# Encoder layer with a mixture of experts on one core: gate weights applied at the experts' eviction, second gather added in the DMA, last norm in two DVE operations

## The chip, the cores and the metric

One core of one Trainium2 chip. The metric is the device time of one execution in microseconds; lower is better. Times of before are the median of three runs, and one further execution was profiled.

## The reference

For 2048 tokens of width 1024, in fp32, one layer with two sub-layers:

```
x = layernorm(x, ln0)
x = layernorm(ALPHA * x + mixer(x), ln1)
group = argmax(x @ w_rg);  two best of the 8 experts in that group
w = softmax(two logits) * softmax(groups)[group]
ffn[token] = sum over its 2 experts of  w * ((silu(x @ w1[e]) * (x @ w3[e])) @ w2[e])
ple = sigmoid(x @ w_ple_gate + b) * (p @ w_ple_proj)
out = layernorm(ALPHA * x + ffn + ple, ln2)
```

There are 32 experts; each token goes to two. The mixer is a gated short convolution and centred pooling between an input and an output projection.

## The kernel before

Every fp32 product is made of three matmuls on TensorE (`mm3`, L222 to L224): each operand is split into a high half (ACT cast, L332) and a low half (subtraction, mostly on DVE, L333), and high x high, high x low and low x high are added up in PSUM. Weights stream through two pools of 128x1024 slots in SBUF, called RB and RY (one allocator, SR); split operands lie in FB.

The work runs in stages. First the norm and the mixer, up to some 560 us. Then the output projection, the second norm and the router of the 16 token tiles. Then, up to a loop at some 730 us, the "embed" products (the `ple` term, `embed_tile`) of six tiles run on TensorE while `dispatch` works out where each token's rows go. Then come the 32 experts, up to some 1450 us, and last the tail: the embed products of the other ten tiles (the list END), beside which `fetch` gathers each token's two expert rows and `finish` forms the last norm.

`dispatch` (L909 to L1014) counts the rows of each expert, ranks experts by size, and gives every (token, choice) a slot number SLI, split into block BLK and position POS. To turn this into a table "which token is in block b at position q" it multiplies matrices: "place" (L1000, one-hot in position, eight tiles in 1024 columns) times "num" (L991, one-hot in block, times the token number at L993), 32 matmuls on TensorE (L1005) that add up in one PSUM bank. TBI and TBH are the tables read from it; gathers of the experts' inputs (L1332, by POOL's queue) use them. Where a token has its rows in the result is known from SLI.

The experts write their results, unweighted, to `yd` in DRAM: ACT copies PSUM to SBUF (L1631; for a half block DVE adds the two halves) and a DMA on POOL's queue stores it.

In the tail, `fetch` (L1735 to L1749) loads for the six early tiles the sum of the other terms (`based`) and gathers two slots of 128x1024 for each tile, from `yd`, with two indirect DMAs on POOL's queue. `finish` then runs for 14 tiles: two weighted additions on DVE (L1783, with the gate weights GW, the second also summing the row), the mean's sign and scale on POOL (L1789), Square with a sum on ACT (L1791), the variance, its power -1/2 and the bias on POOL (L1793 to L1795), the normalisation on ACT (L1797), the multiplication by the norm's weight on DVE (L1798), and the addition of its bias on POOL, or for a quarter of the tiles on DVE (L1799). `finish_last` does the last two tiles in halves, by another form of the norm (`ln_apply`, L328 and L329). L1238, L1243 and L1252 evict the embed products on DVE. The output DMAs stand on ACT's queue.

The order of instructions on every engine is set when the kernel is built, by a planner with costs of its own; generators (`yield`) offer their work to it in pieces. So a change of an operation can move others.

## Time and profile before

| | before |
|---|---|
| median of 3 runs | 1617.14 us (1616.31 to 1617.79) |
| profiled execution | 1620.22 us, its span 1618.6 us |
| TensorE busy | 1550.0 us, 96% of the span |
| DVE, ACT, POOL busy | 1158.9, 792.2, 490.8 us |
| mean granted TensorE clock | 0.982 |
| DMA | 430.63 MB, 266 GB/s |

The busy share of an engine tells only which one has no room; what a stage costs is read from its waits and from the timeline. A matmul's row gives its whole duration, 0.39 us for 512 columns; since matmuls overlap, the distance of two starts (0.23 us) is what one costs. PEclk is the share of full speed that TensorE's clock was granted.

### The profile page before, as it was taken

What the parts mean: (1) busy time and instruction counts of PE and PEld (TensorE: products, weight loads), DVE (VectorE), ACT (ScalarE), POOL (GpSimd) and SP (SyncE); (2) the same over time, 40 slices, a digit from 0 to 9 for tenths busy, and PEclk for the clock granted to TensorE, in tenths of its full rate; (3) what the DMA queues carried; (4) which work ended last, traced back from release to release, by engine and by line L of the source; (5) the groups of instructions that cost most, each with busy time, mean ns of one, the idle gap of its engine ahead of it and who ended that gap; (6) DMA issues with size and microseconds to landing.
All of it is one profiled execution on the core that took longest, in us unless ns stands there. A gap on an engine that the chain in (4) does not pass through costs nothing.

```text
span 1618.6 us, 22474 instructions
## 1 busy us (share of the span) xinstructions
PE 1550.0 (96%) x7770; PEld 1306.8 (81%) x7771; DVE 1158.9 (72%) x1492; ACT 792.2 (49%) x1027; POOL 490.8 (30%) x683
## 2 busy tenths in 40 slices
PE   6999999999999999998999999999999999999895
PEld 5887878887878887777988998988888888878774
DVE  6777484345666667767888878878888767767796
ACT  7343242113111124137778777777787766652332
POOL 3455673441133215110313101111111111007763
PEclk9999999999999999999999999999999999999987
DMA  6547159886386536459788998999998987987961
GB/s 208 183 147 224 63 171 310 335 301 199 108 268 212 169 107 255 139 201 358 280 332 320 401 378 316 355 369 345 355 359 325 329 306 282 384 328 281 357 216 65
DMA packets 205757, 430.63 MB, mean 266 GB/s; under 512 B 19144, under 2 KB 70904, under 8 KB 205640
## 3 DMA queue, kind: packets, MB, share of 16 engines
q1 hardware_dynamic: 162096, 292.33, 50.5%
q0 software_dynamic: 35024, 125.65, 21.1%
q10 hardware_dynamic: 8520, 11.18, 2.0%
q8 instruction: 62, 1.02, 0.2%
q14 instruction: 55, 0.45, 0.1%
HBM read 331.95 MB, written 97.16 MB: 265 GB/s over the span
## 4 chain that ended last, share of the span: by engine, by line
PE 45%; POOL 4%; issue 2%; DVE 2%; ACT 1%; DMA 1%; POOLq 0%; ACTq 0%; DVEq 0%
PE PS L1519 10%; PE PS L222 10%; PE PS L224 10%; PE PS L223 10%; PE PS L339 2%; PE PS L1465 1%; PE PS L1466 1%; POOL RY L1799 1%; PE PS L1589 1%; POOL RY L1746 1%; POOL rstd L1794 1%; POOL rstd L1793 0%; DMA RB<-based 0%; PE PS L1383 0%; POOL RB L1746 0%
## 5 line engine op out<-in xcount | busy, mean ns | idle before, releaser
L223 PE MATMUL PS<-FB 128*128 128x512 f32 (+1 forms) x1356 | 527.3, 389 | 5.5 <-DVE FB L333 5.5
L222 PE MATMUL PS<-FB 128*128 128x512 f32 (+1 forms) x1276 | 497.5, 393 | 15.6 <-DVE FB L333 10.5
L224 PE MATMUL PS<-FB 128*128 128x512 f32 (+1 forms) x1276 | 495.0, 389 | 3.0 <-DVE FB L333 2.9
L333 DVE TENSOR_TENSOR FB<-RY,FB 128x1024 fp32r<-128x1024 f32 x243 | 292.8, 1229 | 53.5 <-ACT FB L332 36.9
L223 PEld LDWEIGHTS PS<-FB 128*128 128x128 f32 x1356 | 258.3, 190 | 56.7 <-DVE FB L333 7.0
L222 PEld LDWEIGHTS PS<-FB 128*128 128x128 f32 x1276 | 242.9, 191 | 65.0 <-DVE FB L333 12.0
L224 PEld LDWEIGHTS PS<-FB 128*128 128x128 f32 x1276 | 242.7, 190 | 52.6 <-DVE FB L333 4.2
L333 DVE TENSOR_TENSOR FB<-RB,FB 128x1024 fp32r<-128x1024 f32 x201 | 241.8, 1218 | 59.3 <-ACT FB L332 46.1
L332 ACT CAST FB<-RY 128x1024 fp32r<-128x1024 f32 x247 | 252.7, 1051 | 60.9 <-PE PS L223 22.9
L332 ACT CAST FB<-RB 128x1024 fp32r<-128x1024 f32 x205 | 211.0, 1049 | 122.9 <-PE PS L223 41.3
L1519 PE MATMUL PS<-FB 128*128 128x296 f32 (+15 forms) x1280 | 175.4, 297 | 6.4 <-ACT FB L332 5.7
L1519 PEld LDWEIGHTS PS<-FB 128*128 128x128 f32 x1280 | 171.3, 191 | 7.8 <-issue 5.9
L332 ACT CAST FB<-PS 128x1024 fp32r<-128x1024 f32 (+9 forms) x142 | 81.7, 592 | 137.6 <-PE PS L339 83.3
L333 DVE TENSOR_TENSOR FB<-PS,FB 128x1024 fp32r<-128x1024 f32 (+9 forms) x142 | 96.0, 689 | 62.2 <-ACT FB L332 61.8
L223 PE MATMUL PS<-FB,FY 128*128 128x512 f32 x264 | 104.1, 394 | 0.0
L1332 POOL DMA_INDIRECT RY<-x1d,TBI x22 | 47.8, 2175 | 173.1 <-DVE FB L333 132.4
L222 PE MATMUL PS<-FB,FY 128*128 128x512 f32 x216 | 85.9, 397 | 0.0
L224 PE MATMUL PS<-FB,FY 128*128 128x512 f32 x216 | 85.4, 395 | 0.0
L1332 POOL DMA_INDIRECT RB<-x1d,TBI x18 | 36.3, 2016 | 156.6 <-DMA RY<-in_w_dram 67.8
L1632 POOL DMA_DIRECT2D yd<-RY x25 | 14.3, 574 | 228.3 <-ACT RY L1631 227.1
L222 PE MATMUL PS<-FY,FB 128*128 128x512 f32 x180 | 71.6, 398 | 0.0
L332 ACT CAST FY<-RB 128x1024 fp32r<-128x1024 f32 (+1 forms) x30 | 31.0, 1035 | 82.8 <-PE PS L223 59.7
(284 smaller groups left out, 2110.0 us busy)
## 6 DMA issues: line engine op xcount, KB each, us to landing
RY<-in_w_dram SPq DMA_DIRECT2D x233, 512.0 KB
RB<-in_w_dram SPq DMA_DIRECT2D x151, 512.0 KB
yd<-RB POOLq DMA_DIRECT2D x67, 512.0 KB, 9.2
RB<-in_w_in_dram SPq DMA_DIRECT2D x32, 512.0 KB
yd<-RY POOLq DMA_DIRECT2D x25, 512.0 KB, 7.0
RB<-in_x_dram SPq DMA_DIRECT2D x24, 512.0 KB
x1Td<-FB POOLq DMA_DIRECT2D x20, 512.0 KB, 5.9
FB<-x1Td SPq DMA_DIRECT2D x20, 512.0 KB
```

What stands on the lines that cost most here:

```text
L222: nc.tensor.matmul(o, ah, bh, start=start, stop=False)
L223: nc.tensor.matmul(o, ah, bl, start=False, stop=False)
L224: nc.tensor.matmul(o, al, bh, start=False, stop=stop)
L332: nc.scalar.copy(hi, src)
L333: eng.tensor_sub(lo, src, hi)
L339: nc.tensor.transpose(v[:, k], src[:, k * 128:(k + 1) * 128], ident)
L1332: nc.gpsimd.indirect_dma_start(out=RB[0:half or 128, rows[n]], out_offset=None, in_=x1d, in_offset=bass.IndirectOffsetOnAxis(ap=idx, axis=0))
L1465: nc.tensor.matmul(o, xs[0][:, c], wh, start=start, stop=False)
L1466: nc.tensor.matmul(o, xs[0][:, c], wl, start=False, stop=stop)
L1519: nc.tensor.matmul(o, u, v, start=k == 0 and q == 0, stop=k == KD - 1 and q == 1)
L1589: nc.tensor.transpose(v[:, k], g[:, k * 128:(k + 1) * 128], ident[0:m, 0:m])
L1746: nc.gpsimd.indirect_dma_start(out=RB[:, yq[t, i]], out_offset=None, in_=yd, in_offset=bass.IndirectOffsetOnAxis(ap=SLI[:, i, t:t + 1], ax ...
```

## The change

Gate weights. In `dispatch` the gate weight of a row goes the same way as its token number: a second set of 40 columns, "gate" = num times GW (L998 of the new file), stands beside num in two neighbouring slots, and the place products are 80 columns wide instead of 40 (L1011). So they are found by position: GWI and GWH hold, for each block, the weight of the row in each partition. The two choices (i = 0, 1) are now handled one after the other, with the pair of slots taken anew for each. The eviction of an expert (L1639 to L1642) multiplies by it: ACT's copy becomes an activation with a scale, DVE's addition a fused multiply-add.

Gathers. As rows come weighted, `fetch` (L1755 to L1772) gathers the first rows of a tile into a slot and then lets the second DMA add its rows into the same slot. The second is issued when the next tile's first one has been.

Norm. `finish` adds the gathered sum and the other terms on DVE with a row sum (L1812), scales the mean on DVE (L1814), forms (a - mean) * weight on DVE (L1815), the Square on ACT (L1816), and the power on POOL (L1818, L1819). One tile later, `end_finish` multiplies by the power and adds the norm's bias in one DVE operation (L1829). ACT's normalisation, L1798, L1799 and two small POOL operations are gone. `finish_last` has one DVE operation in place of an ACT and two DVE operations.

The core of the diff; the wide experts' split (it reads the same elements by another pattern) and the loop for overflowing blocks (which carries the weights too) are left out:

```
@@ -982,16 +986,17 @@
         SZ.free(z1)
         yield
-        num = {}
         for i in range(2):
-            yield from wait(SR)
-            nu = SR.get()
+            yield from wait(SR, 2)
+            nu = SR.get(2)
+            both = RB[:, nu:nu + 2].rearrange("p a c -> p (a c)")[:, :NT * 2 * NB].rearrange("p (t b) -> p t b", b=2 * NB)
+            num, gate = both[:, :, 0:NB], both[:, :, NB:2 * NB]
             eng = nc.gpsimd if i else nc.vector
-            num[i] = nu, RB[:, nu, :NT * NB].rearrange("p (t b) -> p t b", b=NB)
-            nc.vector.tensor_tensor(num[i][1], BLK[:, i, :, None].to_broadcast([128, NT, NB]),
+            nc.vector.tensor_tensor(num, BLK[:, i, :, None].to_broadcast([128, NT, NB]),
                                     io[:, None, 0:NB].to_broadcast([128, NT, NB]), op=OP.is_equal)
-            eng.tensor_tensor(num[i][1], num[i][1], tok[:, :, None].to_broadcast([128, NT, NB]), op=OP.mult)
-        for i in range(2):
+            nc.vector.tensor_tensor(gate, num, GW[:, i, :, None].to_broadcast([128, NT, NB]), op=OP.mult)
+            eng.tensor_tensor(num, num, tok[:, :, None].to_broadcast([128, NT, NB]), op=OP.mult)
             for h in range(2):
                 yield from wait(SR)
                 pl = SR.get()
...
@@ -1002,13 +1007,15 @@
                 yield
                 for t in range(NT // 2):
                     q = h * NT // 2 + t
-                    nc.tensor.matmul(PS[:, b2, 0:NB], place[:, t], num[i][1][:, q], start=i == 0 and q == 0,
-                                     stop=i == 1 and q == NT - 1)
+                    begin, end = i == 0 and q == 0, i == 1 and q == NT - 1
+                    nc.tensor.matmul(PS[:, b2, 0:2 * NB], place[:, t], both[:, q], start=begin, stop=end)
                 SR.free(pl)
                 yield
-            SR.free(num[i][0])
+            SR.free(nu, 2)
         nc.vector.tensor_copy(TBI, PS[:, b2, 0:NB])
         nc.vector.tensor_copy(TBH, PS[64:128, b2, FCUM[NE]:NB])
+        nc.scalar.copy(GWI, PS[:, b2, NB:2 * NB])
+        nc.scalar.copy(GWH, PS[64:128, b2, NB + FCUM[NE]:2 * NB])
         SP.free(b2)
         yield
...
@@ -1623,12 +1632,13 @@
                 SF.free(f)
                 q = take(SR)
                 pv = PS[:, bs[n]:bs[n] + 2].rearrange("p a t -> p (a t)")
+                gw = GWO if n == "o" else blocks[n][3]
                 if len(xs) == 1:
-                    nc.scalar.copy(RB[0:64, q], pv[64:128])
-                    nc.vector.tensor_add(RB[0:64, q], RB[0:64, q], pv[0:64])
-                    nc.gpsimd.dma_start(dst(n), RB[64 - blocks[n][2]:64, q])
+                    nc.scalar.activation(RB[0:64, q], pv[64:128], AF.Copy, scale=gw)
+                    nc.vector.scalar_tensor_tensor(RB[0:64, q], pv[0:64], gw, RB[0:64, q], op0=OP.mult, op1=OP.add)
+                    nc.gpsimd.dma_start(dst(n), RB[0:blocks[n][2], q])
                 else:
-                    nc.scalar.copy(RB[:, q], pv)
+                    nc.scalar.activation(RB[:, q], pv, AF.Copy, scale=gw)
                     nc.gpsimd.dma_start(dst(n), RB[:, q])
                 SP.free(bs[n], 2)
                 SR.free(q)
...
@@ -1740,13 +1753,28 @@
                 yield from wait(SR)
                 base[t] = SR.get()
                 nc.sync.dma_start(RB[:, base[t]], based[t * 128:(t + 1) * 128, :])
-            for i in range(2):
-                yield from wait(SR)
-                yq[t, i] = SR.get()
-                nc.gpsimd.indirect_dma_start(out=RB[:, yq[t, i]], out_offset=None, in_=yd,
-                                             in_offset=bass.IndirectOffsetOnAxis(ap=SLI[:, i, t:t + 1], axis=0))
-                yield
-            start(f"f{t}", finish_last(t) if t in END[-LAST:] else finish(t), 1.0)
+            yield from wait(SR)
+            yq[t] = SR.get()
+            gather_rows(t, 0)
+            yield
+            if len(order) > 1:
+                gather_rows(order[-2], 1)
+                start_finish(order[-2])
+            yield
+        gather_rows(order[-1], 1)
+        start_finish(order[-1])
+    order = []
+    def gather_rows(t, i):
+        if i == 0:
+            order.append(t)
+        nc.gpsimd.indirect_dma_start(out=RB[:, yq[t]], out_offset=None, in_=yd,
+                                     in_offset=bass.IndirectOffsetOnAxis(ap=SLI[:, i, t:t + 1], axis=0),
+                                     compute_op=OP.add if i else OP.bypass)
+    def start_finish(t):
+        start(f"f{t}", finish_last(t) if t in END[-LAST:] else finish(t), 1.0)
     def finish_last(t):
...
@@ -1755,11 +1783,10 @@
         while t not in xs:
             yield
         a = RB[:, base[t]]
-        nc.scalar.mul(a, a, ALPHA)
-        for i in range(2):
-            nc.vector.scalar_tensor_tensor(a, RB[:, yq[t, i]], GW[:, i, t:t + 1], a, op0=OP.mult, op1=OP.add)
-            SR.free(yq.pop((t, i)))
-            yield
+        q = yq.pop(t)
+        nc.vector.scalar_tensor_tensor(a, a, ALPHA, RB[:, q], op0=OP.mult, op1=OP.add)
+        SR.free(q)
+        yield
         summed.append(t)
         while t not in embedded:
             yield
...
@@ -1772,36 +1799,40 @@
             eng.dma_start(outf[t * 128:(t + 1) * 128, cols], a[:, cols])
         SR.free(base.pop(t))
+    waiting = []
     def finish(t):
         for _ in range(6):
             yield
         while t in END and t not in embedded:
             yield
-        a = RB[:, base[t]]
+        a, q = RB[:, base[t]], yq.pop(t)
+        y = RB[:, q]
         s = turn[0] = LAST + (turn[0] - LAST + 1) % (8 - LAST)
-        for i in range(2):
-            nc.vector.scalar_tensor_tensor(a, RB[:, yq[t, i]], GW[:, i, t:t + 1], a, op0=OP.mult,
-                                           op1=OP.add, **({"accum_out": nbias[:, s:s + 1]} if i else {}))
-            if i == 0:
-                SR.free(yq.pop((t, 0)))
-            yield
-        nc.gpsimd.tensor_scalar(nbias[:, s:s + 1], nbias[:, s:s + 1], -1.0 / D, None, op0=OP.mult)
-        q = yq.pop((t, 1))
-        nc.scalar.activation(RB[:, q], a, AF.Square, bias=nbias[:, s:s + 1], accum_out=rstd[:, s:s + 1])
-        SR.free(q)
+        nc.vector.scalar_tensor_tensor(a, y, 1.0, a, op0=OP.mult, op1=OP.add, accum_out=nbias[:, s:s + 1])
+        nc.vector.tensor_scalar(nbias[:, s:s + 1], nbias[:, s:s + 1], -1.0 / D, None, op0=OP.mult)
+        centred = nc.vector.scalar_tensor_tensor(y, a, nbias[:, s:s + 1], RB[:, g2], op0=OP.add, op1=OP.mult)
+        nc.scalar.activation(a, a, AF.Square, bias=nbias[:, s:s + 1], accum_out=rstd[:, s:s + 1])
+        SR.free(base.pop(t))
         nc.gpsimd.tensor_scalar(rstd[:, s:s + 1], rstd[:, s:s + 1], 1.0 / D, EPS, op0=OP.mult, op1=OP.add)
         nc.gpsimd.tensor_tensor(rstd[:, s:s + 1], rstd[:, s:s + 1], mhalf[:, 0:1], op=OP.pow)
-        nc.gpsimd.tensor_tensor(nbias[:, s:s + 1], nbias[:, s:s + 1], rstd[:, s:s + 1], op=OP.mult)
-        yield
-        nc.scalar.activation(a, a, AF.Identity, bias=nbias[:, s:s + 1], scale=rstd[:, s:s + 1])
-        nc.vector.tensor_mul(a, a, RB[:, g2])
-        (nc.gpsimd if t % 4 else nc.vector).tensor_add(a, a, RB[:, b2])
-        for _ in range(8):
-            yield
-        nc.scalar.dma_start(outf[t * 128:(t + 1) * 128, :], a)
-        SR.free(base.pop(t))
-        yield
+        waiting.append((t, q, s))
+        if len(waiting) > 1:
+            end_finish(centred)
+        yield
+    def end_finish(centred=None):
+        t, q, s = waiting.pop(0)
+        y = RB[:, q]
+        last = nc.vector.scalar_tensor_tensor(y, y, rstd[:, s:s + 1], RB[:, b2], op0=OP.mult, op1=OP.add)
+        if centred is not None:
+            tc.add_manual_dep(last.ins, centred.ins.name,
+                              mybir.DependencyInfo(mybir.DependencyClass.NoSync, mybir.DependencyReason.DATA),
+                              reason="in order")
+        nc.scalar.dma_start(outf[t * 128:(t + 1) * 128, :], y)
+        SR.free(q)
     embedded, summed = [], []
     rest = [t for t in range(NT) if t not in END]
...
@@ -1818,8 +1849,11 @@
         run(embed_tile(t, ws))
         embedded.append(t)
         prepare_tile(i + 2)
+        while len(embedded) == len(END) - 1 and waiting:
+            end_finish()
     bg.forget(jobs.pop("split"))
     bg.drain()
+    assert not waiting
 # ---- launch: one core; inputs and outputs as the reference has them ----
```

What this does to the order at three places. First, DVE in the dispatch. Before, from the cast of the slot numbers on (BLK, POS: block and position; tok: token numbers; TBI, TBH: the tables):

```order
L976 CAST SLI<-ZB 128x32
L978 TENSOR_SCALAR ZB<-SLI 128x32
L979 CAST BLK<-ZB 128x32
L980 TENSOR_SCALAR ZB<-SLI 128x32
L991 TENSOR_TENSOR RB<-BLK,io 128x640 x2
L981 CAST POS<-ZB 128x32
L993 TENSOR_TENSOR RB<-RB,tok 128x640
L1000 TENSOR_TENSOR RY<-POS,io 128x1024 x2
L1191 TENSOR_TENSOR ZB<-PS,RB 128x512 x2
L1197 SCALAR_TENSOR_TENSOR ZB<-ZB,PS 128x512
L1000 TENSOR_TENSOR RY<-POS,io 128x1024
L1197 SCALAR_TENSOR_TENSOR ZB<-ZB,PS 128x512
```

and now, from the cast of BLK on (ahead of it stand the slot numbers' cast L980 and two L1198 evictions of the embedding):

```order
L983 CAST BLK<-ZB 128x32
L984 TENSOR_SCALAR ZB<-SLI 128x32
L996 TENSOR_TENSOR RY<-BLK,io 128x16x40
L985 CAST POS<-ZB 128x32
L998 TENSOR_TENSOR RY<-RY,GW 128x16x40
L1005 TENSOR_TENSOR RB<-POS,io 128x1024 x2
L1005 TENSOR_TENSOR RY<-POS,io 128x1024
L999 TENSOR_TENSOR RY<-RY,tok 128x16x40
L1005 TENSOR_TENSOR RB<-POS,io 128x1024
L996 TENSOR_TENSOR RY<-BLK,io 128x16x40
L998 TENSOR_TENSOR RY<-RY,GW 128x16x40
L1015 CAST TBI<-PS 128x40
```

Before, both choices' num matrices (L991) stand ahead of all place matrices; now the first choice's token product (L999) stands behind three place matrices (L1005) and the second choice's num and gate (L996, L998) come last, into the same slots.

Second, TensorE at the place products. Before, the first half of them:

```order
L224 MATMUL PS<-FB 128x512
L1005 MATMUL PS<-RB,RY 128x40 x16
L222 MATMUL PS<-FB 128x512
L223 MATMUL PS<-FB 128x512
L224 MATMUL PS<-FB 128x512
```

and now all of them:

```order
L224 MATMUL PS<-FB 128x512
L1011 MATMUL PS<-RY,RB 128x80 x24
L1011 MATMUL PS<-RY 128x80 x8
L222 MATMUL PS<-FB 128x512
L223 MATMUL PS<-FB 128x512
L224 MATMUL PS<-FB 128x512
```

Before, 18 matmuls of mm3 stand between the two halves of 16; now the 32 follow one another. Counted from the matmul before EOR and the tables (L934 before, L938 now) to the first place product, 76 matmuls of mm3 stood there, and 66 do now; behind the last, up to the first transposes L339 of the gathered rows, 56 stood and 24 do now.

Third, POOL in the tail, early in the finishing of tiles (yd,SLI: gathers; nbias, rstd: the norm's numbers). Before:

```order
L1746 DMA RY<-yd,SLI 128x1024
L1799 TENSOR_TENSOR RY<-RY,RB 128x1024
L1794 TENSOR_TENSOR rstd<-rstd,mhalf 128x1
L1789 TENSOR_SCALAR nbias<-nbias 128x1
L1795 TENSOR_TENSOR nbias<-nbias,rstd 128x1
L1799 TENSOR_TENSOR RB<-RB 128x1024
L1793 TENSOR_SCALAR rstd<-rstd 128x1
L1746 DMA RB<-yd,SLI 128x1024
```

and now:

```order
L1772 DMA RY<-yd,SLI 128x1024
L1772 DMA RB<-yd,SLI 128x1024
L1818 TENSOR_SCALAR rstd<-rstd 128x1
L1772 DMA RY<-yd,SLI 128x1024
L1819 TENSOR_TENSOR rstd<-rstd,mhalf 128x1
L1772 DMA RY<-yd,SLI 128x1024
L1818 TENSOR_SCALAR rstd<-rstd 128x1
L1819 TENSOR_TENSOR rstd<-rstd,mhalf 128x1
L1818 TENSOR_SCALAR rstd<-rstd 128x1
L1772 DMA RY<-yd,SLI 128x1024
```

The additions of 128x1024 (L1799) are gone from POOL's order, and gathers stand between the norm's small operations; every second one waits for the landing of the one that it adds to.

## Rows read from the trace of the kernel before

**Rows 1.** Windows: stretch, length, busy us (count) of PE, PEld, DVE, ACT, POOL; PEclk; DMA

```profile
740.00:1440.00 700.00, 698.28 (x3823) 606.09 (x3822) 562.62 (x624) 512.91 (x657) 110.33 (x83) 1.00 0.91 341
...
1540.00:1550.00 10.00, 8.36 (x26) 6.68 (x27) 9.33 (x13) 4.23 (x6) 8.78 (x10) 0.65 0.58 188
```

**Rows 2.** Waits of PE in 1440 to 1619: total us, times, longest

```profile
PE PS L222 <- DVE FB L333: 9.2, 1, 9.2
```

**Rows 3.** Timeline of DVE, 1528 to 1542: start us, us, engine, line, operation

```profile
1528.03 1.23 DVE L1798 TENSOR_TENSOR RB<-RB 128x1024 f32<-128x1024 f32 x1 [3.66 <-ACT RB L1797]
...
1532.41 2.87 DVE L1798 TENSOR_TENSOR RY<-RY,RB 128x1024 f32<-128x1024 f32 x1 [0.76 <-ACT RY L1797]
...
1535.81 3.37 DVE L1798 TENSOR_TENSOR RY<-RY,RB 128x1024 f32<-128x1024 f32 x1
...
1539.70 1.27 DVE L1783 SCALAR_TENSOR_TENSOR RY<-RY,GW 128x1024 f32<-128x1024 f32 x1
...
1540.90 0.68 DVE L333 TENSOR_TENSOR FB<-PS,FB 128x512 fp32r<-128x512 f32 x1
```

**Rows 4.** Timeline of ACT: a Square just ahead of the cast L332

```profile
1535.40 1.15 ACT L1791 ACTIVATE RB<-RB,nbias 128x1024 f32<-128x1024 f32 x1 [1.90 <-POOL nbias L1789]
```

**Rows 5.** Timeline of POOL, 1531 to 1536

```profile
1531.84 2.36 POOL L1799 TENSOR_TENSOR RB<-RB 128x1024 f32<-128x1024 f32 x1
1534.18 1.19 POOL L1789 TENSOR_SCALAR nbias<-nbias 128x1 f32<-128x1 f32 x1
```

**Rows 6.** Timeline of the end, PE and DVE

```profile
1598.95 0.39 PE L224 MATMUL PS<-FB 128*128 128x512 f32 x1
...
1599.89 1.41 DVE L329 SCALAR_TENSOR_TENSOR RB<-RB,rstd 128x512 f32<-128x512 f32 x2 [0.46 <-POOL rstd L325]
1601.22 1.28 DVE L1238 TENSOR_TENSOR ZB<-PS,RB 128x512 f32<-128x512 f32 x2
```

**Rows 7.** Timeline of PE in the dispatch, 686 to 712

```profile
686.14 3.66 PE L1005 MATMUL PS<-RB,RY 128*128 128x40 f32 x32
...
698.11 0.63 PE L223 MATMUL PS<-FB 128*128 128x512 f32 x1
...
699.82 0.63 PE L224 MATMUL PS<-FB 128*128 128x512 f32 x1
...
711.52 0.39 PE L223 MATMUL PS<-FB 128*128 128x512 f32 x1
711.75 0.60 PE L339 MATMUL PS<-ident,RY 128*128 128x128 f32 x4
```

**Rows 8.** DMA issues, 1440 to 1619: KB each, median us to landing

```profile
RY<-yd,SLI POOLq DMA_INDIRECT x22, 7.0
```

**Rows 9.** Timeline of POOL: the first gather of the tail

```profile
1457.99 0.99 POOL L1746 DMA_INDIRECT RB<-yd,SLI  x1 [8.24 <-DMA FB<-x1Td]
```

**Rows 10.** Timeline of DVE: low half of the third embedded tile's split

```profile
1504.41 0.68 DVE L333 TENSOR_TENSOR FB<-PS,FB 128x512 fp32r<-128x512 f32 x1
```

**Rows 11.** Instructions of line 1631: duration min/median/max ns, first and last start

```profile
L1631 ACT COPY RY<-PS x25: 1002/1016/1035, 775.6 to 1447.9; 128x1024 f32<-128x1024 f32 x25
```

**Rows 12.** Timeline of DVE in the dispatch, 665 to 690

```profile
665.89 0.30 DVE L932 TENSOR_TENSOR ZB<-ZB,TB 32x160 bf16<-32x160 f32 x1
...
668.88 0.19 DVE L939 CAST EOR<-PS 128x32 int32<-128x32 f32 x1
...
678.98 0.18 DVE L976 CAST SLI<-ZB 128x32 int32<-128x32 f32 x1
...
681.28 0.82 DVE L993 TENSOR_TENSOR RB<-RB,tok 128x640 f32<-128x640 f32 x1
...
685.36 1.28 DVE L1191 TENSOR_TENSOR ZB<-PS,RB 128x512 f32<-128x512 f32 x2
...
688.05 1.23 DVE L1000 TENSOR_TENSOR RY<-POS,io 128x1024 f32<-128x1024 f32 x1 [0.63 <-PE PS L1005]
```

**Rows 13.** Timeline of POOL in the dispatch: the token product

```profile
681.36 1.86 POOL L993 TENSOR_TENSOR RB<-RB,tok 128x640 f32<-128x640 f32 x1 [27.02 <-DVE POS L981]
```

## The prediction

> **What bounds the kernel now.** I began with the busy shares of the page: TensorE (PE) is busy 96% of the span, so only time that PE loses or regains reaches the end. Between 740 and 1440 us PE works 698.28 of 700 us [rows 1]: whatever PE loses ahead of the experts arrives at the end one for one, and DVE, ACT and POOL have no say there. Next I asked where PE waits. In the last 180 us there is one wait of weight, 9.2 us [rows 2], and after it the clock is at 0.65 for ten microseconds: 26 matmuls take 8.36 us [rows 1] where at the full pitch of 0.23 (711.52 to 711.75, [rows 7]) they take 5.9. That gap costs 9.2 + 2.5 = 11.7 us.

> Why is it there? PE waits for the low half of a split, DVE L333, which ends at 1541.6. Ahead of it in DVE's queue stand two L1798 multiplies of 2.87 and 3.37 us, where one takes 1.23 alone [rows 3]; both lie beside POOL's L1799 additions. The high half on ACT (L332) stood behind the Square L1791, which waited for POOL's nbias operation, and that was queued behind an L1799 of 2.36 us [rows 4, 5]. So the gap is made of POOL's 1024-wide additions, twice over.

> The last PE matmul ends at 1599.34 and DVE begins on its result only at 1601.22 [rows 6], being still busy with the tile before. That is another 1.5 us or so.

> The third place is the dispatch, at 660 to 700 us. PE does not wait there now: 76 matmuls of mm3 cover the DVE chain, and 18 more stand between the two halves of the place products, 16 matmuls each [rows 7].

> **The tail, part by part.** Each of 14 tiles loses on ACT an Identity pass, on DVE L1798 and three of the additions, on POOL eleven L1799 and the L1789 and L1795 operations. DVE gains two two-tensor operations for them, and loses one of its two weighted sums, which moves into the DMA. DVE's own work so stays about what it was: three passes of some 1.28 us now, against two sums and a multiply before; what goes is the stretching. With no 1024-wide work left on POOL both causes of the gap go: I take the whole 11.7 us, with 7 as the low bound (a wait of 4 to 5 us remains at the same split behind other DVE work) and 12 as the high one. The end gains 1.3 us (0 to 2). Late next in the tail are the gathers.

> The second gather of a tile now starts only when the first has landed, and adds while it lands. No such DMA is in this trace. The plain gathers give 7.0 us to landing [rows 8]; I take the same for the adding one, as the nearest row, and twice, 14 us, as the bound for it. It could be quicker too, but nothing hangs on that side. The first gather is issued at 1458.0 [rows 9]; six first gathers go out at 1.25 us spacing, then the second ones, so the first sum is in SBUF at 1458 + 7.6 + 7.0 = 1472.6. DVE then has the sums of seven tiles, their centring and evictions of the embedding, some 24.5 us by the durations of [rows 3], before the subtraction L333 of the third embedded tile: about 1498. The seventh sum itself needs, from 1472.6, a DVE pass and a Square (2.5), POOL's small operation and issue (2), and two landings in series (14.0): 1491, so DVE's queue ends last. Today that subtraction runs at 1504.41 [rows 10] and PE does not wait for it. Slack is thus about 6 us, and I cost the waits at nothing. Were this cover gone, PE would wait.

> [...]

> **The experts.** 34 evictions on ACT become scaled copies. The copy takes 1.016 us [rows 11], an activation with a bias 1.15 [rows 4]; 0.13 x 34 = 4.6 us of ACT, spread over 700 us in which PE is never short. Nothing (bound 0 to 0.5). The half blocks' fused multiply-add takes the place of an addition of the same width. The overflow loop is not entered.

> **The dispatch.** Here the change costs. Its order puts the two small matmuls L934 and L938 next to each other; the second needs two DVE operations (0.30 us for the second of them, [rows 12]) and handoffs: 0.7 us of waiting. The next mm3 waits for ACT's copy of the table: 0.7 us. Then 66 mm3 follow, 15.0 us. DVE takes from the EOR cast to the SLI cast 10.1 us (668.88 to 678.98), then two L1198 (1.28), three small ones (0.5), the number matrix and the gate product (0.8 each, as L993), three place matrices (3 x 1.2) and the token product (0.8), all from [rows 12]: 17.9 us. Against 15.0 + 0.7 this leaves PE waiting 2.2 us at the first L1011. After its 16th matmul nothing covers: the second half's number and gate matrices go into the slots that the first half has just read, so DVE rebuilds them (0.8 + 0.8) and POOL multiplies (1.86, [rows 13]): 3.6 us with the handoffs. The mm3 behind waits for the two casts and the two ACT copies, 0.7 us. Sum 0.7 + 0.7 + 2.2 + 3.6 + 0.7 = 7.9 us.

> Three costs come on top. Today six mm3 behind the second half run at the slow pitch of 0.43 [rows 7], 1.2 us lost; after idle stretches I expect about what followed the tail's gap, 2.5, so +1.3 (0 to 3.6). Columns go from 40 to 80 in 32 matmuls of 0.23 us (3.66 for 16); I take 0.3, with nothing and 2.1 as bounds. And the gathers of the first expert are issued hardly earlier than today, while their transposes L339 come after 24 mm3 where 56 stood (today at 711.75, [rows 7], without a wait): with 7.0 us to landing PE waits 1 us (0 to 3). The dispatch costs 10.5 us, between 7.9 and 15.

> **Sum.** +10.5 - 11.7 - 1.3 = -2.5 us on the profiled execution's 1620.22, that is 1617.7. The median of the runs lies 3.1 us under that execution, so I forecast 1617.14 - 2.5 = 1614.6. By the bounds the case runs from -5.5 (dispatch 7.9, tail as taken) to +1.5 (dispatch 14.5).

> **Rivals.** *The adding gathers are slow* (slower). Two of them stand in the chain to the seventh sum and six ahead of DVE's first sums; if each takes 14 us, the seventh sum comes at 1505 and the split at about 1509, PE's wait is 5 us, and with the clock behind it 7.5; a second, shorter wait at the next split brings it to 10. It decides from some 4 us per gather beyond 7.0. [...] Against: 6 us of slack. Time: 1614.6 + 10 = 1624.6.

> *The dispatch hides more* (faster). If DVE's chain from EOR to SLI, which no longer has two L1197/L1201 ahead of it, runs two or three microseconds earlier, the wait at the first L1011 goes, and with shorter idle the clock does not fall further: 10.5 becomes 5.5, time 1609.6. Against: the rebuild between the halves has no cover at any timing.

> *The gap stays* (the change doesn't do what it says). If the split waits not for POOL's additions but for whatever finishing work stands ahead of it on DVE and ACT, the new passes take their place: L1829 waits for POOL's power operation, which waits for the Square. PE then still loses 4 to 6 us there, the tail gives 7, and the time is 1617.14 + 10.5 - 7 = 1620.6. For it: DVE's share hardly falls.

> **How the numbers follow.** My forecast has a chance of 0.42, slow gathers 0.22, a better hidden dispatch 0.22, a remaining gap 0.14. About 0.2%, 3.2 us, is what a measurement of this kernel can tell from no change. Of my own case -5.5 to +1.5 lies 0.18 below that bound and 0.24 within; the hidden dispatch is faster; the slow gathers slower; of the remaining gap 0.09 is slower and 0.05 within. Faster 0.40, same 0.29, slower 0.31. Range: from 1607, 2.6 under the faster rival, to 1626, a little over the slower one; less than 2 in 10 is left outside. The likeliest case's own range is 1611.6 to 1618.6.

> **What would show it.** In the profile after: PE's waits at L1011 of some 2 and 3.5 us, both on DVE or POOL operations of the dispatch, and PE reaching the barrier about 10 us later; no 1024-wide POOL operation after 1440 and no PE wait above 2 us on L333 there; DVE passes of 1.28 us throughout; the adding gathers at about 7 us. I am wrong if a wait at an L1812 or at a split behind it shows on PE after 1490, if the L1011 waits are under 1 us, or if PE's gap near 1535 is still there.

## The result, and the profile after

The change makes the kernel slower: 1626.32 us (median of six runs, 1622.26 to 1631.73) against 1615.31 us for the kernel before in the same runs, 11.0 us more; the ratio is 1.0070 (95% interval 1.0053 to 1.0087). The forecast was 1614.6, 2.5 us less than before, with a range from 1607 to 1626: the time lies just over the range's end, and the change goes the other way.

The profiled execution of the changed kernel is its longest, with a span of 1630.1 us, and each table below rests on one execution of each kernel. Spans can't be compared whole here: the same program part reaches the dispatch anywhere between 651 and 663 us in the profiles below. So I cut each profile at five landmarks on TensorE: the first long matmul of the ranking in the dispatch, the first expert matmul behind the loop, the last transposes of the experts, the last matmul, the span's end.

| us | to the ranking | dispatch to the loop's end | experts | tail, to the last matmul | after it |
|---|---|---|---|---|---|
| before | 662.2 | 71.0 | 706.8 | 158.9 | 19.6 |
| after | 661.1 | 83.8 | 708.5 | 161.5 | 15.2 |
| difference | -1.2 | +12.8 | +1.7 | +2.6 | -4.4 |

The dispatch takes 12.8 us more, the stretch behind it 1.7 more. The tail as a whole, which was to give back 13, gives 1.8. So on the two profiles the change costs 11.5 us.

TensorE's waits of the changed kernel from 640 to 735 us (total, times, longest):

```profile
PE PS L1011 <- POOL RY L999: 3.2, 1, 3.2
...
PE PS L1011 <- DVE RY L999: 2.8, 1, 2.8
PE PS L222 <- ACT GWH L1018: 0.9, 1, 0.9
PE PS L222 <- DVE ZB L952: 0.8, 1, 0.8
PE PS L938 <- DVE ZB L936: 0.7, 1, 0.7
```

These are the five waits that the prediction named: 3.2, 2.8, 0.9, 0.8 and 0.7, together 8.4 us. (The row left out, 2.9 us, lies ahead of the ranking.) There is more. The place products of the changed kernel on TensorE's timeline (start us, us; the trace has two records for each of these fp32 products, so x32 are 16 products):

```profile
684.29 5.18 PE L1011 MATMUL PS<-RY,RB 128*128 128x80 f32 x32 [2.83 <-DVE RY L999]
692.65 3.71 PE L1011 MATMUL PS<-RY,RB 128*128 128x80 f32 x16 [3.18 <-POOL RY L999]
696.15 3.62 PE L1011 MATMUL PS<-RY 128*128 128x80 f32 x16
700.71 0.79 PE L222 MATMUL PS<-FB 128*128 128x512 f32 x1 [0.94 <-ACT GWH L1018]
701.30 0.63 PE L223 MATMUL PS<-FB 128*128 128x512 f32 x1
```

The first half of 16 products takes 5.2 us (684.29 to 689.5), the second 7.1 (692.65 to 699.8), where the two halves took 3.66 ([rows 7]) and 3.9 before. The windows say why (busy us and counts of PE, PEld, DVE, ACT, POOL; PEclk; DMA share; GB/s):

```profile
684.00:690.00 6.00, 5.18 (x32) 4.99 (x32) 1.86 (x3) 0.00 (x0) 0.00 (x0) 0.70 0.00 1
692.00:700.00 8.00, 7.12 (x32) 6.90 (x32) 0.19 (x1) 0.00 (x0) 0.60 (x1) 0.50 0.35 118
700.00:707.00 7.00, 6.29 (x15) 4.93 (x16) 1.40 (x3) 2.12 (x4) 2.96 (x3) 0.51 0.92 317
```

Before, the first half took its 3.66 us with 1.00 granted (686 to 690); at 0.50 a half should take twice that, 7.3 us, and the second half takes 7.1. The granted clock, 1.00 over 676 to 684, falls during the first half, after the wait of 2.8 us, and stays low past 706 (0.51 over 700 to 707): fourteen mm3 follow at the slow pitch, 0.43 us from start to start against 0.23 behind them, where there were six. Behind the loop it is the clock again: over the first 40 us of the experts 0.88 was granted (744.9 to 784.9) where it was 0.94 before (733.3 to 773.3), which by these shares is some 2.4 us (an estimate), against the 1.7.

In the tail PE waits at four places again (timeline, only rows with a wait):

```profile
1520.12 0.50 PE L222 MATMUL PS<-FB 128*128 128x512 f32 x1 [2.69 <-DVE ZB L1250]
...
1537.56 0.33 PE L1139 MATMUL PS<-ident,RY 128*128 128x128 f32 x1 [2.08 <-DVE ZB L1250]
...
1557.00 0.80 PE L222 MATMUL PS<-FB 128*128 128x512 f32 x1 [6.02 <-DVE FB L333]
...
1563.80 0.66 PE L1139 MATMUL PS<-ident,RY 128*128 128x128 f32 x4 [1.40 <-DVE ZB L1250]
```

Together 12.2 us, against the one of 9.2 [rows 2]. DVE shows what they wait for. Its timeline, with the idle time ahead of an operation and its releaser in brackets:

```profile
1488.71 1.23 DVE L1812 SCALAR_TENSOR_TENSOR RY<-RB,RY 128x1024 f32<-128x1024 f32 x1 [11.05 <-DMA RB<-yd,SLI]
...
1491.47 1.23 DVE L1812 SCALAR_TENSOR_TENSOR RY<-RB,RY 128x1024 f32<-128x1024 f32 x1 [0.27 <-DMA RB<-yd,SLI]
...
1495.71 1.28 DVE L1812 SCALAR_TENSOR_TENSOR RY<-RY 128x1024 f32<-128x1024 f32 x1 [1.21 <-DMA RY<-yd,SLI]
...
1499.41 1.23 DVE L1812 SCALAR_TENSOR_TENSOR RY<-RB,RY 128x1024 f32<-128x1024 f32 x1 [1.74 <-DMA RB<-yd,SLI]
...
1503.26 1.23 DVE L1812 SCALAR_TENSOR_TENSOR RY<-RY 128x1024 f32<-128x1024 f32 x1 [2.01 <-DMA RY<-yd,SLI]
...
1518.23 1.23 DVE L1812 SCALAR_TENSOR_TENSOR RY<-RY 128x1024 f32<-128x1024 f32 x1 [2.18 <-DMA RY<-yd,SLI]
...
1520.58 0.68 DVE L333 TENSOR_TENSOR FB<-PS,FB 128x512 fp32r<-128x512 f32 x1
```

The first six sums L1812 come some 3 to 4 us apart, five of them after a wait for their adding gathers. The seventh waits until 1518.2; behind it stand L1250, with which TensorE's wait of 2.7 us ends, and L333, the split that TensorE needs next. The longest wait, 6.0 us, has the same form two sums later:

```profile
1548.98 1.23 DVE L1812 SCALAR_TENSOR_TENSOR RY<-RB,RY 128x1024 f32<-128x1024 f32 x1 [7.16 <-DMA RB<-yd,SLI]
...
1555.11 1.23 DVE L1812 SCALAR_TENSOR_TENSOR RY<-RY 128x1024 f32<-128x1024 f32 x1
...
1556.26 0.68 DVE L333 TENSOR_TENSOR FB<-PS,FB 128x512 fp32r<-128x512 f32 x1
```

DVE sits idle for 7.2 us until an adding gather has landed, and the split stands behind that sum and the one after it. POOL's order holds the reason for the seventh sum (the first and the second gather of that tile):

```profile
1495.74 0.98 POOL L1772 DMA_INDIRECT RY<-yd,SLI  x1 [0.27 <-issue]
...
1507.19 1.80 POOL L1772 DMA_INDIRECT RY<-yd,SLI  x1 [9.75 <-DMA RY<-yd,SLI]
```

The second is issued 11.5 us after the first, when that one has landed; the sum starts 11.0 us later still.

What became better is what was forecast for POOL and for the end: no 1024-wide operation is left on POOL in the tail, DVE's passes take 1.22 to 1.31 us (against 2.87 and 3.37 in [rows 3]), and DVE begins on the last matmuls' result at once: 15.2 us from the last matmul's start to the end, where it was 19.6.

### The profile page after: what moved, and what is told of

Same layout as the page of the kernel before. It is cut to its first block, busy times and chain, and to the rows that moved or that the text cites. A ratio compares the mean times of both kernels' runs of the same rounds, so it can differ in the third digit from the quotient of the medians.

```text
span 1630.1 us, 22402 instructions
## 1 busy us (share of the span) xinstructions
PE 1556.3 (95%) x7770; PEld 1312.2 (81%) x7771; DVE 1141.0 (70%) x1503; ACT 778.2 (48%) x1013; POOL 448.1 (27%) x644
## 4 chain that ended last, share of the span: by engine, by line
PE 47%; DMA 4%; POOL 1%; DVE 1%; issue 1%; ACT 0%; POOLq 0%; DVEq 0%; ACTq 0%
PE PS L222 10%; PE PS L224 10%; PE PS L223 10%; PE PS L1527 10%; DMA RB<-yd,SLI 2%; PE PS L339 2%; PE PS L1474 1%; PE PS L1473 1%; DMA RY<-yd,SLI 1%; PE PS L1598 1%; DMA out_dram<-RB 1%; POOL RB L1772 0%; DMA FB<-x1Td 0%; POOL RY L1772 0%; PE PS L1390 0%
## 5 line engine op out<-in xcount | busy, mean ns | idle before, releaser
L333 DVE TENSOR_TENSOR FB<-RY,FB 128x1024 fp32r<-128x1024 f32 x237 | 286.3, 1230 | 60.6 <-ACT FB L332 43.7
L333 DVE TENSOR_TENSOR FB<-RB,FB 128x1024 fp32r<-128x1024 f32 x207 | 249.8, 1218 | 55.4 <-ACT FB L332 46.0
L332 ACT CAST FB<-RY 128x1024 fp32r<-128x1024 f32 x241 | 247.3, 1050 | 59.6 <-PE PS L223 22.1
L332 ACT CAST FB<-RB 128x1024 fp32r<-128x1024 f32 x211 | 218.5, 1049 | 119.6 <-PE PS L223 39.7
L333 DVE TENSOR_TENSOR FB<-PS,FB 128x1024 fp32r<-128x1024 f32 (+9 forms) x142 | 96.1, 690 | 67.7 <-ACT FB L332 63.8
L332 ACT CAST FB<-PS 128x1024 fp32r<-128x1024 f32 (+9 forms) x142 | 82.2, 592 | 127.0 <-PE PS L339 81.0
L1339 POOL DMA_INDIRECT RY<-x1d,TBI x26 | 58.2, 2237 | 227.1 <-DVE FB L333 154.2
L222 PE MATMUL PS<-FY,FB 128*128 128x512 f32 x180 | 71.7, 398 | 0.0
L332 ACT CAST FY<-RB 128x1024 fp32r<-128x1024 f32 (+1 forms) x30 | 31.0, 1035 | 83.5 <-PE PS L223 59.7
L224 PE MATMUL PS<-FY,FB 128*128 128x512 f32 x180 | 70.7, 394 | 0.0
L324 POOL TENSOR_SCALAR rstd<-mv 128x1 f32<-128x1 f32 x42 | 29.3, 700 | 148.9 <-DVE mv L319 114.6
```

Source lines behind the costliest of these rows:

```text
L222: nc.tensor.matmul(o, ah, bh, start=start, stop=False)
L224: nc.tensor.matmul(o, al, bh, start=False, stop=stop)
L324: nc.gpsimd.tensor_scalar(rstd[:, s:s + 1], mv[:, s, 1:2], EPS, None, op0=OP.add)
L332: nc.scalar.copy(hi, src)
L333: eng.tensor_sub(lo, src, hi)
L1339: nc.gpsimd.indirect_dma_start(out=RB[0:half or 128, rows[n]], out_offset=None, in_=x1d, in_offset=bass.IndirectOffsetOnAxis(ap=idx, axis=0))
```

## The experiments

Theories stand in the expectations: A, adding costs DMA time; B, the serial pair of gathers does; C, the new norm holds TensorE up; D, the rebuild of num and gate between the halves of the place products costs; E, the longer chain and the planner's order do. Runs 1 to 6 and 9 were timed against the kernel before on the same chip. Their profiles and that of run 8, cut at the landmarks of above:

| us | dispatch to the loop's end | experts | tail, to the last matmul | after it |
|---|---|---|---|---|
| 1 no adding | 83.8 | 708.2 | 150.2 | 15.2 |
| 2 plain gathers | 83.9 | 708.3 | 151.9 | 15.2 |
| 3 norm alone | 70.7 | 706.8 | 146.8 | 16.9 |
| 4 gates alone | 83.7 | 708.5 | 155.6 | 17.2 |
| 5 num and gate ahead | 80.4 | 707.9 | 146.4 | 15.2 |
| 6 serial, no gate | 70.2 | 707.4 | 156.4 | 19.0 |
| 8 narrow products | 83.7 | 707.9 | 157.6 | 15.2 |
| 9 work between | 82.8 | 705.9 | 146.4 | 15.2 |

**1. No adding.** The edit:

```
-compute_op=OP.add if i else OP.bypass)
+compute_op=OP.bypass)
```

> The changed kernel with the second gather overwriting the first rows instead of adding to them (the first expert's rows are left out of the result); the order of instructions on TensorE, DVE and POOL is the same as in the changed kernel. Theory A (an adding gather costs the DMA engines more time than a plain one, and they are full in the tail): landings come 1.5 to 2.5 us apart instead of 3.7, PE's waits in the tail fall from some 13 us to under 7, time 1617 to 1621 us. Theory B (not the adding, but that a tile's second gather waits for its first): unchanged, 1624 to 1628 us.

Measured: 1615.34 us, ratio to before 1.0006 (0.9995 to 1.0016): 10.3 us less than the changed kernel by the ratios and 11.0 by the medians, with the same order on three engines, and 1.7 us under the expected range. The tail takes 150.2 us instead of 161.5, and DVE's waits for gathers at L1812 fall from 29.6 to 13.5 us. TensorE's waits from 1425 on:

```profile
PE PS L222 <- DMA FB<-x1Td: 2.0, 1, 2.0
PE PS L1139 <- ACT RY L1641: 0.8, 1, 0.8
PE PS L1139 <- DVE ZB L1250: 0.7, 1, 0.7
```

The share of the DMA engines that the gathers' queue took from 1480 to 1510 (packets, MB, share of 16 engines over 30 us), first in the changed kernel:

```profile
q0 software_dynamic: 1518, 5.50, 74.8%
```

and without the add:

```profile
q0 software_dynamic: 1555, 5.65, 52.8%
```

The changed kernel moves 5.50 MB in 22.4 us of all engines, 245 GB/s; without the add 5.65 MB take 15.8 us, 357 GB/s. Over 1440 to 1600 the same queue takes 43.2% and 32.2% of the engines for 18.35 MB: 17.6 us for 16 adds of 0.5 MB, 1.1 us each. All queues together kept the DMA engines busy to 0.92 in that stretch, as the last two columns of the window show (DMA share, GB/s; without the add 0.80):

```profile
1440.00:1600.00 160.00, 146.24 (x642) 118.61 (x641) 107.62 (x144) 47.74 (x69) 64.17 (x62) 0.98 0.92 294
```

Without the add the median to landing is 7.7 us over all 32 gathers and the longest 13.7; the trace of the changed kernel gives a landing for 8 of its 32 alone, with 9.4 and 18.5 us. Theory A holds. B doesn't: the second gather waits for the first here too.

**2. Plain gathers.** Two slots for each tile, no wait between the gathers, one more DVE sum:

```
+            for i in range(2):
+                yield from wait(SR)
+                yq[t, i] = SR.get()
+                nc.gpsimd.indirect_dma_start(out=RB[:, yq[t, i]], ...)
...
+        nc.vector.scalar_tensor_tensor(a, RB[:, yq[t, 0]], 1.0, a, op0=OP.mult, op1=OP.add)
```

> The changed kernel with plain gathers into two slots, issued one behind the other without a wait, and one more DVE sum for each tile; gate tables, scaled evictions and the new norm stay. Theories A and B both: the tail's PE waits fall under 5 us, the dispatch keeps its 11.6 us; time 1613 to 1618 us. Theory C (the new norm's order on DVE and ACT is what holds TensorE in the tail): the waits stay above 10 us, time 1622 to 1627 us.

Measured: 1617.49 us, ratio 1.0019 (1.0008 to 1.0030). The tail takes 151.9 us, with one wait of 3.6 us left at L333 and 5.1 us of waits in all, just over the 5 expected; the dispatch keeps 83.9. The time lies within the range of A and B, and C is out. It is no faster than the first run, though no gather waits for the other; as it has one DVE sum more for each tile, it can't say alone what the pair's order costs.

**3. The new norm alone.** The kernel before with `finish` in the new form, gate weights and plain gathers as they were:

```
+        nc.vector.scalar_tensor_tensor(a, RB[:, yq[t, 0]], GW[:, 0, t:t + 1], a, op0=OP.mult, op1=OP.add)
+        nc.vector.scalar_tensor_tensor(a, y, GW[:, 1, t:t + 1], a, op0=OP.mult, op1=OP.add, accum_out=nbias[:, s:s + 1])
+        nc.vector.tensor_scalar(nbias[:, s:s + 1], nbias[:, s:s + 1], -1.0 / D, None, op0=OP.mult)
+        centred = nc.vector.scalar_tensor_tensor(y, a, nbias[:, s:s + 1], RB[:, g2], op0=OP.add, op1=OP.mult)
```

> The kernel before with the new norm alone (two DVE operations, no 1024-wide work on POOL), two plain gathers and gate weights applied in the tail; the dispatch and the experts' eviction are as before. As the prediction had it (the gap of 9.2 us is made by POOL's additions): the gap goes, 1602 to 1607 us. Theory C (the gap moves to the new operations): 1612 to 1617 us.

Measured: 1599.07 us, ratio 0.9898 (0.9882 to 0.9913), 15.5 us less than before, faster than both kernels and 2.9 us under the expected range. The dispatch takes 70.7 us, the tail 146.8 and 16.9. TensorE's waits from 1425 on:

```profile
PE PS L222 <- ACT FB L332: 1.2, 1, 1.2
PE PS L1132 <- ACT RY L1631: 0.7, 1, 0.7
```

The gap of 9.2 us is gone, and nothing took its place. Theory C is out, and the old norm is shown to have made the gap. That it was POOL's additions in it, as the prediction had it, isn't shown by itself, since ACT's pass and a DVE multiplication went with them. The trace of before speaks for it: of five L1798 beside an addition of POOL four take 2.87 to 3.98 us, the others 1.2.

**4. The gates alone.** Tables by place and scaled evictions, plain gathers, the old norm with a factor of 1 (`GW[:, i, t:t + 1]` becomes `1.0` in `finish`).

> The kernel before with the gate weights alone: tables found by place, scaled evictions, plain gathers, the old norm with POOL's additions. If what TensorE loses in the dispatch passes to the end one for one: 1625 to 1629 us, with the waits at L1011 of 2.8 and 3.2 us. If part of it is hidden behind the loop or the experts' loads: 1617 to 1621 us.

Measured: 1623.75 us, ratio 1.0055 (1.0042 to 1.0068). The waits at L1011 are 3.2 and 2.8 us again, the dispatch takes 83.7 and the experts 708.5: the loss passes one for one. The total is 1.3 us under the expected range because the tail with its end takes 5.8 us less than before in this order; its gap is 5.9 us instead of 9.2, and `finish_last` has its new form (tail 155.6 and 17.2).

**5. Num and gate of both choices ahead.** On the kernel of run 2:

```
+        both, nus = {}, {}
         for i in range(2):
             yield from wait(SR, 2)
+            nu = nus[i] = SR.get(2)
...
+            eng.tensor_tensor(num, num, tok[:, :, None].to_broadcast([128, NT, NB]), op=OP.mult)
         for i in range(2):
             for h in range(2):
```

> The kernel of the second run (plain gathers) with num and gate of both choices built ahead, in slots of their own, as the kernel before does with num. Theory D (the rebuild between the halves of the place products costs the wait of 3.2 us and lets the clock fall): no wait between the halves; from the ranking's first matmul to the loop's end 76 to 79 us instead of 83.8; time 1610 to 1613 us. Theory E (the longer DVE chain with gate, and the planner's order without mm3 between the halves, cost it in any case): PE waits 5 us or more at the first place product instead, 82 to 84 us, time 1615 to 1619 us.

Measured: 1608.92 us, ratio 0.9957 (0.9941 to 0.9974); the dispatch takes 80.4 us. The dispatch lies between the two theories: the wait of 3.2 us and no more is gone. The time lies under both ranges, because the planner ordered the tail anew too: 146.4 us instead of 151.9 in run 2, without the wait of 3.6. The place products on PE's timeline:

```profile
680.17 9.49 PE L1013 MATMUL PS<-RY,RB 128*128 128x80 f32 x48 [2.91 <-DVE RY L1000]
689.45 3.62 PE L1013 MATMUL PS<-RY 128*128 128x80 f32 x16
```

and a window over them (columns as above):

```profile
684.00:690.00 6.00, 6.00 (x30) 6.00 (x30) 1.31 (x2) 0.00 (x0) 0.00 (x0) 0.50 0.44 150
```

Without the pause in the middle the 32 products still take 12.9 us (680.17 to 693.1) instead of 7.6, with 0.77 granted over 678 to 684 and 0.50 over 684 to 694. So D explains 3.4 us, and the larger rest is the clock and the first wait of 2.9 us.

**6. The serial order without gate.** On the kernel before, num built anew for the second choice in one slot (`num` taken and freed inside the loop over i, no gate).

> The kernel before with the two choices one after the other in the dispatch, num taken anew for each in one slot, and no gate. Theory D: the rebuild alone costs 4 us or more, 1619 to 1624 us. Theory E: without gate the planner finds cover (22 mm3 stand between the halves in its order), the stretch stays within 2 us of before, 1613 to 1617 us.

Measured: 1612.47 us, ratio 0.9986 (0.9973 to 0.9999); the dispatch takes 70.2 us. Theory E, by 0.5 us under its range in time: without gate the planner keeps 21 mm3 between the halves, each half takes 3.66 us, as the first did before ([rows 7]), and the rebuild costs nothing.

**7. A probe of the adding DMA.** On the kernel before, eight gathers of 128 rows more, ahead of the dispatch, four plain and four adding, read by nobody (the diff's core):

```
+        for again in range(4):
+            for w in range(2):
+                probe_rows(pr + w, again)
```

> The kernel before with eight gathers of 128 rows more, ahead of the dispatch: two plain ones into two slots, twice, then two adding ones into the same slots, twice; their result is read by nobody. If adding costs engine time (theory A): a pair of adding gathers takes the DMA engines 1.6 to 2 times a plain pair, with or without other traffic. If it only lands later: the same engine time and 2 us or more of latency.

Measured, one execution: 1617.09 us. Time to landing, min, median and max, of the four plain gathers:

```profile
DMA to landing us min/median/max: 4.4/5.7/6.3
```

and of the four adding ones:

```profile
DMA to landing us min/median/max: 6.9/9.0/11.3
```

The software queue's packets, MB and share of the engines, from 637 to 652 us (plain gathers):

```profile
q0 software_dynamic: 472, 1.74, 35.1%
```

and from 662 to 668 (adding ones, nearly alone):

```profile
q0 software_dynamic: 342, 1.27, 97.4%
```

1.74 MB in 5.3 us of all engines are 330 GB/s; 1.27 MB in 5.8 us are 217 GB/s. Here adding costs 1.5 times the engine time, a little under the expected 1.6, and 3.3 us more to landing at the median; of the four the two that ran nearly alone have a median of 7.7 us. So it is dear by itself, and not only in the tail's traffic. In the tail it is dearer: a plain gather of 0.5 MB at the 357 GB/s of run 1 takes 1.5 us of all engines, and 1.1 more make some 1.75 times that (an estimate from these two figures).

This run's place products, 40 columns wide, show one thing more. The planner left no mm3 between their halves, and they start without a wait:

```profile
690.61 3.66 PE L1024 MATMUL PS<-RB,RY 128*128 128x40 f32 x32
694.10 6.90 PE L1024 MATMUL PS<-RY 128*128 128x40 f32 x32
```

with windows ahead of them and over the second half:

```profile
684.00:690.00 6.00, 6.00 (x28) 4.95 (x27) 6.00 (x11) 0.56 (x2) 1.26 (x1) 1.00 0.00 0
...
694.00:701.00 7.00, 7.00 (x35) 6.85 (x34) 2.45 (x2) 1.04 (x1) 0.00 (x0) 0.52 0.87 310
```

TensorE is busy without a gap ahead of them and on them, and yet the clock falls with the second half, to 0.52 granted over 694 to 701; that half takes 6.9 us instead of 3.66, and six mm3 behind it run at the slow pitch.

**8. Narrow products.** The changed kernel with `PS[:, b2, 0:NB]` and `num[:, q]` in the place products, 40 columns wide.

> The changed kernel with place products 40 columns wide, as before: DVE still forms the gate matrices, but the gate weights read at the end are wrong. TensorE's order up to the tail is that of the changed kernel. If the 80 columns cost TensorE time: the products of the two halves (5.2 and 7.3 us in the changed kernel) shrink by 2 us or more together. If the time there is the clock's (halves with 0.70 and 0.50 granted): they stay within 0.5 us, and the granted clock too.

Measured, one execution: 1622.76 us. The products on its timeline, and a window that holds most of the second half:

```profile
679.86 6.11 PE L1011 MATMUL PS<-RY,RB 128*128 128x40 f32 x32 [2.83 <-DVE RY L999]
689.16 3.64 PE L1011 MATMUL PS<-RY,RB 128*128 128x40 f32 x16 [3.18 <-POOL RY L999]
692.59 3.61 PE L1011 MATMUL PS<-RY 128*128 128x40 f32 x16
```

```profile
692.00:700.00 8.00, 7.11 (x27) 6.39 (x28) 0.37 (x2) 0.35 (x2) 2.10 (x3) 0.50 0.75 238
```

The halves take 6.1 and 7.0 us, together not less than with 80 columns (5.2 and 7.1). The first is 0.9 us longer, outside the 0.5 expected, because there the clock fell earlier: 0.80 was granted over 676 to 684 and 0.50 over 684 to 690, which puts the fall some 0.9 us behind the first product's start, against 2.1 in the changed kernel (an estimate from the windows, with 1.00 ahead of the fall and 0.50 behind it). The width costs nothing; the time there is the clock's. The tail has the same adding gathers in a slightly different order and takes 157.6 us, 3.9 less than the profile of the changed kernel.

**9. Work between the products.** On the kernel of run 5, four fp32 matmuls of 512 columns that nobody reads:

```
+                if not i and not h:
+                    spare = SP.get()
+                    for t in range(4):
+                        nc.tensor.matmul(PS[:, spare], place[:, t % 8], RB[:, pl, 0:512], start=True, stop=True)
+                    SP.free(spare)
```

> The kernel of the fifth run (num and gate built ahead, plain gathers) with four matmuls of 128x512 in full fp32 more, some 3.5 us, on the first place matrix, into a PSUM bank that nobody reads; with them the planner keeps mm3 of the embedding ahead of and between the halves, so that the 32 place products no longer stand in a row. If idle time and the row of narrow products cost it the clock: no wait of over 1 us at the place products, halves of some 3.7 us at full clock, and from the ranking's first matmul to the loop's end 74 to 77 us with the 3.5 us that were added, against 80.4; time 1603 to 1607 us. If the clock falls by the narrow products whatever stands between them: 81 us or more, 1609 to 1613 us.

Measured: 1607.66 us, ratio 0.9951 (0.9932 to 0.9969). The added matmuls (L1012) and the halves on PE's timeline:

```profile
672.26 3.70 PE L1012 MATMUL PS<-RB 128*128 128x512 f32 x8
...
679.48 3.69 PE L1018 MATMUL PS<-RY,RB 128*128 128x80 f32 x32
...
684.89 1.91 PE L1018 MATMUL PS<-RY,RB 128*128 128x80 f32 x16
686.64 1.95 PE L1018 MATMUL PS<-RY 128*128 128x80 f32 x16
```

and the windows over them:

```profile
671.00:684.00 13.00, 12.93 (x67) 9.62 (x66) 7.80 (x9) 0.63 (x1) 3.31 (x1) 1.00 0.01 2
684.00:690.00 6.00, 5.06 (x39) 4.70 (x38) 1.06 (x3) 0.98 (x3) 0.88 (x1) 1.00 0.82 285
```

The halves take 3.7 and 3.7 us with 1.00 granted and without a wait: the products themselves don't force the slow clock. The time is 0.7 us over the expected range, and the stretch of 82.8 us is well over it, but 18 mm3 (4.1 us) that stood ahead of the ranking now stand behind it, and the ranking itself ran with 0.50 granted (650 to 656) after a wait of 3.3 us for OH, the one-hot choices that it counts; 78.7 us without the 18. From the first place product on, where run 5 had 57.2 us to the loop's end, this one has 54.4 with 26 mm3 (5.9 us) more to do. The total gains only 1.3 us on run 5, with intervals that overlap: the place is shown, the profit isn't.

## Why the prediction was wrong

**The bounds of the kernel** were read rightly: every loss on TensorE ahead of the experts reached the end (runs 4 and 5), and the gap in the tail was the old norm's (run 3).

**The tail's gain** of 13.0 us was right in its sum for what the change does to the norm: without the add the tail with its end takes 165.4 us against 178.5 before, 13.1 less (run 1); the new norm alone gives 14.8 (run 3). That the sum fits so well is partly luck: the stretch to the last matmul gave 8.7 us where I had 11.7 for the gap, the end 4.4 where I had 1.3 with 2 as the bound. The end varies, too: it takes 17.4 us in run 7, whose tail has the code of before.

**The adding gathers** are the step that failed, "I cost the waits at nothing". I took 7.0 us to landing from the plain gathers, with 14 as the bound, and had 6 us of slack. The runs show a cost in throughput that I did not count at all: 1.1 us more of all 16 engines for each add, in a stretch whose DMA engines are 92% busy. The first six sums came some 3 to 4 us apart, the seventh at 1518.2, or 1504.9 without the 13.3 us by which the experts ended later, where I had 1491. The sign that I had named, a wait at a split behind an L1812 after 1490, came. The term measures 11.3 us on the tail to the last matmul (161.5 against 150.2), 7.4 if the tail of run 8 is taken, and 10.3 to 11 on the time. The first rival was nearest, with 10 us and a chance of 0.22; its 1624.6 lies 1.7 us from the median. That it came so close is in part luck: it had slow landings where the runs show engine time, 5 us at the split behind the seventh sum, where 2.7 fell, and a dispatch that was too cheap. I should have given it more: the DMA engines were 0.83 busy from 1450 to 1500 us already before, and nothing in the trace spoke for an add at the price of a copy.

```profile
1450.00:1500.00 50.00, 50.00 (x224) 41.36 (x223) 32.35 (x37) 12.20 (x18) 33.99 (x34) 1.00 0.83 303
```

The order of the pair, the second gather behind the first one's landing, ran in run 1 too: its tail takes 150.2 us, against 151.9 in run 2, whose gathers don't wait and which has one DVE sum more for each tile, so no cost of this order alone shows here.

**The dispatch** was forecast at 10.5 us between 7.9 and 15, and took 12.8 up to the loop's end and 1.7 behind it. The waits were right: 8.4 us for 7.9. Two small terms were not: width (0.3, with 2.1 as its bound, estimates of mine that no trace showed) is nothing (run 8), and no wait at the gathered rows' transposes showed (1 forecast). The clock was mis-sized, +1.3 within 0 to 3.6: the products took 12.3 instead of 7.6 us and the fourteen slow mm3 1.6 us more than the six, 6.3 in all. I had counted it only behind the products, never on them. These terms make 14.7; of the 1.9 us between them and 12.8, 1.3 is a wait ahead of the loop that only the kernel before has, and some 0.5 are four transposes that now stand ahead of the ranking. The bounds of the sum hold a slip as well: 7.9 - 13.0 is -5.1 and not -5.5, and with the dispatch's own bound of 15 the other end is +2.0.

**The cause inside the dispatch.** Not the rebuild as such, of which I had written that it has no cover at any timing: in run 6 the planner covers it. With the gate's DVE work the planner leaves no mm3 among the 32 products. Moving the rebuild gave 3.4 us (run 5); work between the products gave the clock back (run 9). Run 9 removes the wait ahead of the products and their standing in a row together, but run 7 has the row without a wait, and the clock falls there too (0.52 over 694 to 701): the row is enough. With the wait it falls earlier, in the first half (0.70 granted over 684 to 690 after, 0.77 over 678 to 684 in run 5, 0.80 over 676 to 684 in run 8), and in the changed kernel more mm3 behind are slow, fourteen against run 7's six. What a wait does by itself stays open: one of 2.3 to 2.9 us ahead of the ranking, with mm3 behind it, is followed by some 3 us of slow mm3 in the profiles of before (0.51 granted over 656.1 to 659.2), after (0.53 over 655.5 to 658.8) and run 5 (0.43 us from start to start up to 653.8), and by none in those of runs 1, 2, 6 and 8 (0.23 throughout).

**Evictions with a scale** were costed at nothing. The experts' stretch is 708.5 us in run 4 and 707.9 in run 5 against 706.8. In the changed kernel, with 708.5 as well, the lower clock behind the loop (0.88 granted over 40 us, against 0.94) is some 2.4 us by the estimate of above and covers that, so no run speaks against it.

## What to carry to other kernels

An add in the DMA was no free work moved off an engine here: price it as engine time of the DMA, in these runs 1.5 times a copy nearly alone (run 7) and by estimate some 1.75 times in the tail, whose DMA engines were 0.92 busy, and look at how busy the DMA is where it will run, before asking what DVE saves. When one change carries several ideas, split it: here the norm alone gives 15.5 us, and the two parts that came with it cost more than that. And where a planner sets the order, look for narrow matmuls that end up in a row, above all behind a wait: here 32 of them took 12.3 to 13.2 us when 0.50 was granted on most of them (after, runs 5 and 8), and 7.4 at 1.00 (run 9).
